# Eight block loads of each weight pair: from two with each of four pieces to one about every second piece

## The chip, the cores and the metric

The kernel runs on one core of one Trainium2 chip, in one launch. The metric is the device time in microseconds (us); before the change it is 2352.64 us, the median of three runs (2350.16 to 2354.2).

The core's engines run side by side and each works through its own list in order: PE multiplies matrices, ACT (ScalarE) and DVE (VectorE) do elementwise work, POOL (GpSimd) issues DMA transfers that add to their destination, SP (SyncE) issues nearly all other transfers. An instruction waits on semaphores until what it needs is there. A transfer that SP cannot issue yet holds up all those behind it.

## The reference, cut to what matters

A trunk of two layers on x of 256 tokens by 2048, in float32. Each layer adds a mixer and an MLP; the change touches the two MLPs.

```python
def squared_relu_mlp(h, w_up, w_down):
    u = jnp.einsum('bsd,df->bsf', h, w_up)
    return jnp.einsum('bsf,fd->bsd', jnp.square(jax.nn.relu(u)), w_down)

for layer in range(2):
    x = x + mixer(rms_norm(x, norm_mix[layer]))        # layer 0: windowed attention and Mamba-2, layer 1: dilated attention
    x = x + squared_relu_mlp(rms_norm(x, norm_ffn[layer]), w_up[layer], w_down[layer])
```

w_up is 2048 x 8192 and w_down 8192 x 2048, so each MLP reads 134 MB of weights.

## The kernel before

The kernel streams all weights from HBM through SBUF. Its work is a list, `plan`, of pieces. A piece is two k-tiles (2 x 128 rows) by up to 512 columns of a weight: a tile of 128 x 1024 float32, 512 KB. ACT writes a rounded copy of it (`whi`), DVE the rest (`wlo` = tile - `whi`), and PE multiplies the high and low parts with the high and low parts of the activations, three products in place of one, which keeps float32 accuracy.

There are two sorts of pieces.

- A plain piece (`Unit`) has its tile `wraw` from a ring of four, and takes 12 matmuls of 512 columns into `acc`. The MLP's w_up is done so ("up pieces").
- A pair piece belongs to a `Seven`. It takes the product of 1024 rows and 1024 columns of w_down as a 2 x 2 block product in seven multiplications rather than eight (Winograd's form of Strassen's scheme). Its four weight blocks "11", "12", "21", "22" come in two halves h of 512 KB each, so eight loads `sraw`. The seven multiplications P1, P2, Q3, Q7, Q6, Q5, Q4, two halves each, make 14 pieces of 6 matmuls into banks `sp`, which DVE adds to the residual `res` (`evict`). Sums of blocks that the scheme needs are made in place: by DVE (`add`), and by four accumulating DMAs that POOL issues (`accumulate`): block 22 onto "12" as soon as "12" is loaded, and block 12 onto "11" after P1 has been split.

Each MLP has seven periods c. In the first six, a first pair (columns 0 to 1023) and a second pair (1024 to 2047) are spread among 18 or 19 up pieces by `mixed`: first about five up pieces alone, then pair pieces and up pieces in turn, about two to one. The seventh has one pair among pieces of w_down. That makes 13 pairs a layer, 26 in all, with 208 loads and 104 accumulates.

The order on every engine is written out by hand: the loop in `run` goes over the list once, and at step i it records `low(i + 2)` (DVE), `fetch(i + 6)` (SP), `high(i + 3)` (ACT), `add(i + 4)` (DVE), and PE's matmuls of piece i. So SP's order of transfers is the order of the `fetch` calls, while each transfer goes out as soon as its buffer is free. A `wraw` buffer is free when DVE has split its fourth predecessor. The `sraw` buffers come from a pool of 31 that activations and intermediate results share. Before the change, `fetch` of a pair's piece issues loads with P1 and P2 only: "12" and "11" with either half of P1, "21" and "22" with either half of P2.

Nearly all instructions show line 71, a helper that records them; the SP loads are at L260 (`sraw`) and L307 (`wraw`), the accumulates at L274.

Of the kernel before, what the change touches and what calls it, by code (L numbers as in the profile page):

```python
# [20 lines left out]
W = 512  # L21
KC = 2
# [18 lines left out]
def trunk(ctx: ExitStack, tc: tile.TileContext, x, norm_mix, norm_ffn, w_up, w_down, ab_w_in, ab_q_norm,  # L41
          ab_k_norm, ab_sinks, ab_conv_w, ab_conv_b, ab_dt_bias, ab_a_log, ab_d_skip, ab_gate_norm,
          ab_w_out, c_w_qkv, c_q_norm, c_k_norm, c_w_o, shapes, out):
    nc = tc.nc
# [38 lines left out]
    def aux(name):  # L83
        return auxs.tile([128, W], F32, name=name, tag="aux")

    def f32(ap):
        return ap.bitcast(F32)
# [12 lines left out]
    def load_x(j):  # L100
        nc.sync.dma_start(res[:, :, j * W:(j + 1) * W], xt[:, :, j * W:(j + 1) * W])
# [85 lines left out]
    def need(label):  # L187
        while label not in done:
            assert step(True) or label in done, label
# [43 lines left out]
    def unit(*a, **k):  # L233
# [3 lines left out]

    SEVEN = (("P1", "a", "11"), ("P2", "b", "21"), ("Q3", "d", "22"), ("Q7", "c", "12"), ("Q6", "a", "22"),
             ("Q5", "a", "11"), ("Q4", "c", "21"))
    LOADS = {"P1": ("12", "11"), "P2": ("21", "22")}  # L240
    SUMS = {"Q6": ("22", "11", "22"), "Q4": ("21", "21", "22")}

    class Seven:
# [10 lines left out]
            self.raw[b, h] = t = work.tile([128, KC, W], F32, name="sraw", tag="w4")  # L254
            return t

        def fetch(self, p, h):
            for b in LOADS.get(SEVEN[p][0], ()):
                r, c = self.rows[int(b[0]) - 1] + h * KC, self.c0 + (int(b[1]) - 1) * W
                nc.sync.dma_start(self.tile(b, h),  # L260
                                  self.w[r * 128:(r + KC) * 128, c:c + W].rearrange("(k p) c -> p k c", p=128))
                if b == "12":
                    self.accumulate("12", 1, h)

        def add(self, p, h):
            if SEVEN[p][0] in SUMS:
# [25 lines left out]
    def run():  # L292
        todo = plan
        raws, parts = {}, {}

        def fetch(i):
            if i >= len(todo):
                return
            u, c = todo[i]
            if isinstance(u, Seven):  # L300
                u.fetch(*c)
                return
            kt = u.ktiles[c][0]
            raws[i] = raw = wpool.tile([128, KC, u.n], F32, name="wraw", bufs=RAW)
            o = 0
            for w, c0, m in u.segs:
                nc.sync.dma_start(raw[:, :, o:o + m],  # L307
                                  w[kt * 128:(kt + KC) * 128, c0:c0 + m].rearrange("(k p) c -> p k c", p=128))
                o += m

        def add(i):
            if i < len(todo) and isinstance(todo[i][0], Seven):
                todo[i][0].add(*todo[i][1])

        def high(i):
            if i < len(todo):
                u, c = todo[i]
                if isinstance(u, Seven):
                    raws[i] = u.source(*c)
                raw = raws[i]  # L320
                hi = wpool.tile([128, KC, raw.shape[2]], F32R, name="whi", bufs=AHEAD + 2)
                S.activation(hi, raw, AF.Copy)
                parts[i] = [hi]

        def low(i):
            if i < len(todo):
                raw = raws.pop(i)
                lo = wpool.tile([128, KC, raw.shape[2]], F32R, name="wlo", bufs=AHEAD + 1)
                V.tensor_tensor(lo, raw, f32(parts[i][0]), op=OP.subtract)
                parts[i].append(lo)  # L330
                u, c = todo[i]
                if isinstance(u, Seven) and c[0] == 0:
                    u.accumulate("11", 0, c[1])

        for i in range(RAW):
            if i % 2 == 0:
                load_x(i // 2)
            fetch(i)
        for i in range(AHEAD):
            high(i)  # L340
            low(i)
            if i == 0:
                need(todo[0][0].needs[0])
            if i % 2 == 0:
                load_x(2 + i // 2)
            fetch(RAW + i)
        high(AHEAD)
        nc.sync.dma_start(cst[:, C_TRI:], shapes[:, C_TRI:C_M0])
        nc.sync.dma_start(mask0, shapes[:, C_M0:C_M1])
        pending = []  # L350
        before = ps = None
        kept, held = [], []
        for i, (u, c) in enumerate(todo):
            if i:
                low(i + AHEAD - 1)
                fetch(i + AHEAD - 1 + RAW)
                high(i + AHEAD)
                add(i + AHEAD + 1)
            for f in pending:
                f()  # L360
            pending = []
            hi, lo = parts.pop(i)
            if isinstance(u, Seven):
                p, h = c
                name, b, _ = SEVEN[p]
                if p in u.needs and h == 0:
                    need(u.needs[p])
                new = b not in u.bank
                if new:
                    u.bank[b] = aux("sp")  # L370
                sp = u.bank[b]
                xh, xl, th, tl = u.operands(name)
                tick(True)
                for k in range(KC):
                    q = h * KC + k
                    wh, wl = xh[:, q, th:th + 128], xl[:, q, tl:tl + 128]
                    PE.matmul(sp, wh, hi[:, k], start=new and k == 0, stop=False, skip_group_check=True)
                    PE.matmul(sp, wh, lo[:, k], start=False, stop=False, skip_group_check=True)
                    PE.matmul(sp, wl, hi[:, k], start=False, stop=q == u.halves * KC - 1, skip_group_check=True)
                if h == u.halves - 1:  # L380
                    pending.append(lambda u=u, p=p: u.evict(p))
                    if p == 6:
                        done.add(u.mark)
                continue
            segs, ktiles, flip, n = u.segs, u.ktiles, u.flip, u.n
            if c == 0:
                if before is not None:
                    need(before)
                before = ps and id(ps)
                ps = [accs.tile([128, W], F32, name="acc") for _ in range(2)]  # L390
                kept.append(ps)
            if c in u.needs:
                need(u.needs[c])
            end = i == len(todo) - 1
            for k in range(KC):
                tick()
                first, last = c + k == 0, c + k == len(ktiles) - 1
                xh, xl, j = ktiles[c + k][1]()
                xh, xl = xh[:, j], xl[:, j]
                if flip:  # L400
                    for b in range(n // 128):
                        o = ps[b // 2][:, (b % 2) * T:(b % 2 + 1) * T]
                        wh, wl = hi[:, k, b * 128:(b + 1) * 128], lo[:, k, b * 128:(b + 1) * 128]
                        PE.matmul(o, wh, xh, start=first and b % 2 == 0, stop=False, skip_group_check=True)
                        PE.matmul(o, wh, xl, start=False, stop=False, skip_group_check=True)
                        PE.matmul(o, wl, xh, start=False, stop=last, skip_group_check=True)
                else:
                    rows = [(t, k, xh, xl) for t in range(2)]
                    if end:
                        held += rows  # L410
                        rows = sorted(held, key=lambda r: r[:2]) if last else []
                    for t, q, xh, xl in rows:
                        o = ps[t][:, :n]
                        h, l = xh[:, t * 128:(t + 1) * 128], xl[:, t * 128:(t + 1) * 128]
                        PE.matmul(o, h, hi[:, q], start=first, stop=False)
                        PE.matmul(o, h, lo[:, q], start=False, stop=False)
                        PE.matmul(o, l, hi[:, q], start=False, stop=last and q == k)
            if c + KC >= len(ktiles):
                pending.append(lambda u=u, ps=ps: u.after(ps))
                if u.mark is not None:  # L420
                    done.add(u.mark)
        for f in pending:
            f()
# [727 lines left out]

    mlp(1, n3, None, last=store)
    run()


# [47 lines left out]
```

## Time and profile before

| | |
|---|---|
| median of three runs | 2352.64 us |
| profiled execution | 2353.53 us, its span 2351.7 us |
| mean granted TensorE clock | 0.988 |
| PE, DVE, ACT, POOL busy | 2279.3, 1785.0, 1294.3, 133.8 us |
| read from HBM | 475.17 MB, 203 GB/s over the span |
| block loads by SP | 208 of 512 KB, median 9.1 us from issue to landing |
| accumulates by POOL | 104 of 512 KB, median 9.7 us |
| w_up tiles by SP | 256 of 512 KB, median 4.8 us |

ACT splits the first block of a pair at 535.6 us and the last at 2323.0 us. In a row of waits stand who waits, for whom, the total in us, how many times, and the longest; in a row of stretches the length, the busy time of each engine with its instructions, the granted share of the TensorE clock, the mean busy share of the 16 DMA engines and what they moved. Matmuls are pipelined: one is shown as busy for about 0.39 us while the next starts 0.23 us after it.

### The profile page before, as it was taken

To read this page: it belongs to the slowest core of one execution; us is meant where nothing else is said; L and a number is where in the kernel's file an instruction comes from. 1 tells how busy PE (TensorE), PEld (TensorE's weight loads), DVE (VectorE), ACT (ScalarE), POOL (GpSimd) and SP (SyncE) were. 2 spreads that over 40 slices of the span, in tenths; PEclk is the share of its full clock that TensorE was granted. 3 is DMA by queue.
4 is the path that set the end of the run, shared out by engine and by line. 5 is a ranking of instruction groups with operands and counts; after the bars stand their busy time and mean duration, and the time that the engine had idled before them with its cause. 6 is when DMAs were issued, how large, how long until landed. Compare 5 with 4: busy or idle time off the path is not lost.

```text
span 2351.7 us, 30275 instructions
## 1 busy us (share of the span) xinstructions
PE 2279.3 (97%) x11005; PEld 1882.3 (80%) x11005; DVE 1785.0 (76%) x2534; ACT 1294.3 (55%) x1627; POOL 133.8 (6%) x124
## 2 busy tenths in 40 slices
PE   8999999999999999999999999999999999999999
PEld 7999988888877878777788778778877877778777
DVE  6779886558887978778876776755687888878786
ACT  6565555446555655555554555554565555555553
POOL 1000000001000011001000000000101001011000
PEclk9999999999999999999999999999999999999999
DMA  7546555569687696878656455446969688696973
GB/s 229 163 136 196 179 179 183 186 192 291 189 238 224 193 290 175 254 214 251 179 168 189 159 154 177 155 162 187 277 174 285 188 235 247 167 298 183 272 204 128
DMA packets 257782, 479.29 MB, mean 204 GB/s; under 512 B 17316, under 2 KB 28112, under 8 KB 257632
## 3 DMA queue, kind: packets, MB, share of 16 engines
q1 hardware_dynamic: 219264, 416.34, 54.7%
q0 software_dynamic: 28800, 54.68, 13.0%
q10 hardware_dynamic: 9568, 6.34, 0.9%
q8 instruction: 86, 1.41, 0.2%
q14 instruction: 64, 0.52, 0.1%
HBM read 475.17 MB, written 2.13 MB: 203 GB/s over the span
## 4 chain that ended last, share of the span: by engine, by line
PE 82%; DMA 12%; DVE 4%; ACT 1%; issue 1%; SPq 0%; ACTq 0%; DVEq 0%
PE acc L71 59%; PE sp L71 17%; DMA sraw<-in_w_down_dram 6%; DMA wraw<-in_w_up_dram 5%; DVE wlo L71 2%; PE uT L71 1%; PE sc L71 1%; DVE res L71 1%; PE o L71 1%; ACT whi L71 1%; PE pT L71 1%; PE yp L71 1%; DMA wraw<-in_ab_w_in_dram 1%; PE xT L71 0%; DVE sraw L71 0%
## 5 line engine op out<-in xcount | busy, mean ns | idle before, releaser
L71 DVE TENSOR_TENSOR wlo<-wraw,whi 128x1024 fp32r<-128x1024 f32 (+1 forms) x584 | 705.4, 1215 | 259.7 <-PE acc L71 151.2
L71 ACT ACTIVATE whi<-wraw 128x1024 fp32r<-128x1024 f32 (+1 forms) x584 | 614.4, 1054 | 518.1 <-PE acc L71 291.8
L71 PE MATMUL acc<-whi,hThi 128*128 128x512 f32 (+1 forms) x1632 | 654.4, 401 | 12.8 <-ACT whi L71 10.7
L71 PE MATMUL acc<-wlo,hThi 128*128 128x512 f32 (+1 forms) x1632 | 640.1, 392 | 6.6 <-DVE wlo L71 6.5
L71 PE MATMUL acc<-whi,hTlo 128*128 128x512 f32 (+1 forms) x1632 | 639.9, 392 | 0.6 <-DVE hTlo L71 0.6
L71 ACT ACTIVATE whi<-sraw 128x1024 fp32r<-128x1024 f32 x364 | 382.3, 1059 | 345.8 <-DVE sraw L71 117.4
L71 DVE TENSOR_TENSOR wlo<-sraw,whi 128x1024 fp32r<-128x1024 f32 x364 | 443.7, 1222 | 124.4 <-ACT whi L71 48.4
L71 PEld LDWEIGHTS acc<-whi,hThi 128*128 128x128 f32 x1632 | 310.7, 190 | 81.1 <-ACT whi L71 13.9
L71 PEld LDWEIGHTS acc<-wlo,hThi 128*128 128x128 f32 x1632 | 310.8, 190 | 70.7 <-DVE wlo L71 10.5
L71 PEld LDWEIGHTS acc<-whi,hTlo 128*128 128x128 f32 x1632 | 309.8, 190 | 66.0 <-DVE hTlo L71 1.5
L274 POOL DMA_DIRECT2D sraw<-in_w_down_dram x104 | 125.3, 1208 | 2134.5 <-DMA sraw<-in_w_down_dram 1215.4
L71 PE MATMUL sp<-whi,sh 128*128 128x512 f32 x416 | 165.0, 397 | 22.4 <-DVE res L71 22.4
L71 PE MATMUL sp<-wlo,sh 128*128 128x512 f32 x416 | 164.3, 395 | 0.4
L71 PE MATMUL sp<-whi,sl 128*128 128x512 f32 x416 | 163.6, 393 | 0.0
L71 DVE TENSOR_TENSOR res<-res,sp 128x512 f32<-128x512 f32 x208 | 140.2, 684 | 25.5 <-PE sp L71 24.2
L71 DVE TENSOR_TENSOR sraw<-sraw 128x1024 f32<-128x1024 f32 x104 | 126.9, 1220 | 0.0
L71 PEld LDWEIGHTS sp<-whi,sh 128*128 128x128 f32 x416 | 79.0, 190 | 44.8 <-ACT whi L71 23.7
L71 PE MATMUL acc<-hThi,whi 128*128 128x256 f32 x384 | 112.5, 293 | 0.0
L71 PE MATMUL acc<-hTlo,whi 128*128 128x256 f32 x384 | 108.7, 283 | 0.0
L71 PE MATMUL acc<-hThi,wlo 128*128 128x256 f32 x384 | 108.7, 283 | 0.0
L71 PEld LDWEIGHTS sp<-wlo,sh 128*128 128x128 f32 x416 | 79.0, 190 | 18.5 <-DVE wlo L71 2.6
L71 PEld LDWEIGHTS sp<-whi,sl 128*128 128x128 f32 x416 | 79.2, 190 | 16.5
(227 smaller groups left out, 2790.5 us busy)
## 6 DMA issues: line engine op xcount, KB each, us to landing
wraw<-in_w_up_dram SPq DMA_DIRECT2D x256, 512.0 KB, 4.8
sraw<-in_w_down_dram SPq DMA_DIRECT2D x208, 512.0 KB, 9.1
sraw<-in_w_down_dram POOLq DMA_DIRECT2D x104, 512.0 KB, 9.7
wraw<-in_ab_w_in_dram SPq DMA_DIRECT2D x96, 512.0 KB, 3.7
wraw<-in_c_w_qkv_dram SPq DMA_DIRECT2D x96, 512.0 KB, 4.0
wraw<-in_ab_w_out_dram SPq DMA_DIRECT2D x48, 512.0 KB, 3.6
wraw<-in_w_down_dram SPq DMA_DIRECT2D x48, 512.0 KB, 4.0
wraw<-in_c_w_o_dram SPq DMA_DIRECT2D x32, 512.0 KB, 3.7
```

The source lines that it names most:

```text
L71: return f(out, *a, **k)
L274: nc.gpsimd.dma_start(self.raw[b, h], self.w[r * 128:(r + KC) * 128, c:c + W].rearrange("(k p) c -> p k c", p=128), accum_op=OP.add)
```

## The change

The table LOADS now names the eight loads one by one, with the step at which each is issued, counted from the pair's first piece: "11" half 0 at -12, "11" half 1 at -10, "21" at -8 and -6, "12" at -5 and -3, "22" at -2 and 0. `run` finds each pair's first piece in the list and notes the loads by step; in the step they stand after the `fetch` of the piece six ahead. `fetch` of a pair's piece does nothing now. The accumulate onto "12" is still recorded right behind the load of "12".

```diff
-    LOADS = {"P1": ("12", "11"), "P2": ("21", "22")}
+    LOADS = (("11", 0, -12), ("11", 1, -10), ("21", 0, -8), ("21", 1, -6), ("12", 0, -5), ("12", 1, -3), ("22", 0, -2),
+             ("22", 1, 0))
...
-        def fetch(self, p, h):
-            for b in LOADS.get(SEVEN[p][0], ()):
-                r, c = self.rows[int(b[0]) - 1] + h * KC, self.c0 + (int(b[1]) - 1) * W
-                nc.sync.dma_start(self.tile(b, h),
-                                  self.w[r * 128:(r + KC) * 128, c:c + W].rearrange("(k p) c -> p k c", p=128))
-                if b == "12":
-                    self.accumulate("12", 1, h)
+        def fetch(self, b, h):
+            r, c = self.rows[int(b[0]) - 1] + h * KC, self.c0 + (int(b[1]) - 1) * W
+            nc.sync.dma_start(self.tile(b, h), self.w[r * 128:(r + KC) * 128, c:c + W].rearrange("(k p) c -> p k c", p=128))
+            if b == "12":
+                self.accumulate("12", 1, h)
...
+        blocks = {}
+        for i, (u, c) in enumerate(todo):
+            if isinstance(u, Seven) and c == (0, 0):
+                for b, h, o in LOADS:
+                    blocks.setdefault(i + o, []).append((u, b, h))
...
             if isinstance(u, Seven):
-                u.fetch(*c)
                 return
...
+            for w, b, h in blocks.get(i, ()):
+                w.fetch(b, h)
```

PE, ACT, DVE and POOL have the same instructions in the same order before and after. Only SP's order differs. Its rows for the second period of layer 0 (c = 1), from the end of the period before to past the first pair's loads, were these (`sraw` is a block load, `wraw` an up tile):

```order
L307 DMA wraw<-in_w_up_dram 128x2x512 x10
L260 DMA sraw<-in_w_down_dram 128x2x512 x4
L307 DMA wraw<-in_w_up_dram 128x2x512
L260 DMA sraw<-in_w_down_dram 128x2x512 x4
L307 DMA wraw<-in_w_up_dram 128x2x512 x6
```

They are now:

```order
L310 DMA wraw<-in_w_up_dram 128x2x512 x5
L260 DMA sraw<-in_w_down_dram 128x2x512
L310 DMA wraw<-in_w_up_dram 128x2x512 x2
L260 DMA sraw<-in_w_down_dram 128x2x512
L310 DMA wraw<-in_w_up_dram 128x2x512 x2
L260 DMA sraw<-in_w_down_dram 128x2x512
L310 DMA wraw<-in_w_up_dram 128x2x512
L260 DMA sraw<-in_w_down_dram 128x2x512 x2
L310 DMA wraw<-in_w_up_dram 128x2x512
L260 DMA sraw<-in_w_down_dram 128x2x512 x2
L310 DMA wraw<-in_w_up_dram 128x2x512
L260 DMA sraw<-in_w_down_dram 128x2x512
```

Three of the eight loads have moved ahead of the tenth up tile, which stood right before all eight; the other five stand among the next tiles, two, two and one. For the second pair of the same period SP had eight loads in two blocks of four:

```order
L307 DMA wraw<-in_w_up_dram 128x2x512 x6
L260 DMA sraw<-in_w_down_dram 128x2x512 x4
L307 DMA wraw<-in_w_up_dram 128x2x512
L260 DMA sraw<-in_w_down_dram 128x2x512 x4
L307 DMA wraw<-in_w_up_dram 128x2x512 x10
```

and now has, from behind the first pair's last load on:

```order
L310 DMA wraw<-in_w_up_dram 128x2x512 x3
L260 DMA sraw<-in_w_down_dram 128x2x512
L310 DMA wraw<-in_w_up_dram 128x2x512
L260 DMA sraw<-in_w_down_dram 128x2x512 x2
L310 DMA wraw<-in_w_up_dram 128x2x512
L260 DMA sraw<-in_w_down_dram 128x2x512 x2
L310 DMA wraw<-in_w_up_dram 128x2x512
L260 DMA sraw<-in_w_down_dram 128x2x512 x2
L310 DMA wraw<-in_w_up_dram 128x2x512
L260 DMA sraw<-in_w_down_dram 128x2x512
```

Its first load follows the third up tile behind the first pair's last load, and four up tiles stand among its eight loads where one did.

## The prediction

> **What bounds the kernel now.** I read the page's first lines, then what PE waits for, then a table of stretches around every place where it waits, and last the DMA work there.
>
> ```profile
> span 2351.7 us, 30275 instructions
> PE 2279.3 (97%) x11005; PEld 1882.3 (80%) x11005; DVE 1785.0 (76%) x2534; ACT 1294.3 (55%) x1627; POOL 133.8 (6%) x124
> PE sp L71 <- DVE res L71: 22.4, 16, 2.4
> PE acc L71 <- ACT whi L71: 10.7, 9, 2.7
> PE sp L71 <- DVE wlo L71: 6.7, 9, 0.8
> PE acc L71 <- DVE wlo L71: 6.5, 9, 0.8
> PE uT L71 <- ACT relu L71: 4.8, 2, 4.3
> PE sp L71 <- ACT whi L71: 4.3, 3, 2.9
> ACT whi L71 <- DMA wraw<-in_w_up_dram: 77.6, 32, 7.3
> ACT whi L71 <- DMA sraw<-in_w_down_dram: 69.0, 30, 7.0
> ```
>
> TensorE is busy 97% of the span. What it waits for falls in two kinds: 22.4 us for evictions of a pair's bank (res), and 33.0 us (10.7 + 6.7 + 6.5 + 4.8 + 4.3) for weights that ACT and DVE have not yet split, or for an ACT op queued behind such a split. ACT in its turn waits 146.6 us for weights of these two stages to land. So there is DMA behind the second kind. The next table has ten stretches, one for each period of the two MLPs but the first of each, just where a period's first pair begins. The columns are length, PE busy, granted clock, DMA share and GB/s; two of the ten rows are left out, the sum holds them.
>
> ```profile
> 646.00:662.00 16.00, 11.65 (x33) 0.68 0.78 233
> 744.00:758.00 14.00, 9.31 (x33) 0.88 0.94 283
> 841.00:856.00 15.00, 12.07 (x43) 0.89 0.89 263
> 944.00:956.00 12.00, 9.68 (x39) 1.00 0.95 298
> 1046.00:1056.00 10.00, 7.11 (x28) 1.00 0.95 313
> 1782.00:1796.00 14.00, 8.85 (x28) 0.76 0.77 239
> 1879.00:1895.00 16.00, 11.64 (x36) 0.68 0.82 241
> ...
> 2179.00:2188.00 9.00, 6.67 (x25) 1.00 1.01 332
> sum 126.00, PE 92.58; mean PE 9.26
> ```
>
> PE idles 126.00 - 92.58 = 33.4 us there: all of the second kind. And in five of them the granted clock drops after the pause; at half clock the loss is (1 - clock) x length, 5.1 + 1.7 + 1.7 + 3.4 + 5.1 = 16.9 us. That the slow part is real shows in the chain of work (start, length), in the last two rows of the next fence: twelve matmuls took 5.06 us at 656 and 2.76 us at 664.
>
> ```profile
> 624.70 7.05 DMA sraw<-in_w_down_dram
> 631.81 21.23 DMA wraw<-in_w_up_dram
> 656.32 5.06 PE acc L71 x12
> 664.57 2.76 PE acc L71 x12
> ```
>
> The rows above them say why: a tile of w_up, issued at 631.81, landed 21.23 us later, where the usual is 4.8:
>
> ```profile
> wraw<-in_w_up_dram SPq DMA_DIRECT2D x256, 512.0 KB, 4.8
> sraw<-in_w_down_dram SPq DMA_DIRECT2D x208, 512.0 KB, 9.1
> sraw<-in_w_down_dram POOLq DMA_DIRECT2D x104, 512.0 KB, 9.7
> 620.00:625.00 5.00, 5.00 (x26) 4.15 (x25) 4.58 (x5) 3.68 (x4) 0.00 (x0) 1.00 0.30 97
> 630.00:635.00 5.00, 5.00 (x24) 4.15 (x23) 4.96 (x7) 1.49 (x2) 2.28 (x2) 1.00 1.05 374
> 640.00:645.00 5.00, 5.00 (x24) 4.14 (x23) 2.47 (x3) 1.06 (x1) 1.20 (x1) 1.00 1.10 261
> 650.00:655.00 5.00, 3.17 (x7) 1.86 (x7) 2.58 (x3) 2.32 (x4) 0.00 (x0) 0.59 1.05 385
> 655.00:660.00 5.00, 4.90 (x14) 3.74 (x15) 4.13 (x5) 4.63 (x6) 0.00 (x0) 0.50 0.46 132
> ```
>
> The last two columns are DMA share and GB/s. Before 625 the DMA engines are a third used; from 625 to 655 they are full; after it idle again. A 0.524 MB tile alone takes 0.524/385 = 1.36 us; while POOL's accumulating transfers run, the rate falls to 261, so one of them and one plain tile take 4.0 us together. The burst is eight block loads, four accumulates and, by SP's order, six w_up tiles: 4 x 4.0 + 10 x 1.36 = 29.6 us and some 4 us of first latency, from 624 to 657, as the table shows. This is a queue, not a lack of bandwidth: over the span the mean is 203 GB/s (the table ahead of this).
>
> **The change, part by part.** PE, ACT, DVE and POOL keep their orders; SP issues the same loads in other places. Nothing is added.
>
> ```profile
> L71 DVE TENSOR_TENSOR wlo<-wraw,whi 128x1024 fp32r<-128x1024 f32 (+1 forms) x584 | 705.4, 1215 | 259.7 <-PE acc L71 151.2
> L71 ACT ACTIVATE whi<-wraw 128x1024 fp32r<-128x1024 f32 (+1 forms) x584 | 614.4, 1054 | 518.1 <-PE acc L71 291.8
> ```
>
> (a) The burst. Of a first pair's eight loads, three (11 both halves, 21 first half) now stand before the up tile that opens the burst (issued at about 624), in the stretch that is a third used. That takes 3 x 1.36 = 4.1 us from the burst. More counts for the tile that PE paused for: behind the opening tile it was 11th (1, four loads, 1, four loads, itself) and is now 7th. Until about 635 transfers run at the plain rate, so 5 more land after the first (at 628), and the 7th about one shared step of 4.0 later, at 639, not 653. PE is busy without a break to 645 and has about two pair pieces (2 x 1.4, half of 2.76 each) ahead of it, so wants it at 648 or so; ACT and DVE need 1.05 + 1.22 us (the rows above) before that, so it is some 7 us early. Bounds: above, all of 33.4 + 16.9 less about 2.5 where the half clock lies in a pause and is counted twice, 48; below, each window's loss less 4.1 alone, which leaves 5.4 + 2.3 + 0.5 + 4.4 + 5.4 = 18, so a gain of 32. I take 46, near the upper end, because of the place in the queue.
>
> (b) What follows a pause. DVE had nothing to split meanwhile, and has to catch up; some 20 us later an eviction comes late.
>
> ```profile
> 867.00:877.00 10.00, 7.62 (x29) 0.83 1.08 305
> 2001.00:2011.00 10.00, 7.62 (x29) 0.83 1.08 313
> sum 31.00, PE 21.92; mean PE 5.48
> 822.00:876.00 54.00, 48.69 (x202) 38.71 (x201) 39.78 (x40) 28.80 (x32) 7.22 (x6) 0.94 1.00 295
> 1056.00:1080.00 24.00, 23.13 (x103) 18.85 (x102) 22.44 (x23) 14.77 (x17) 2.41 (x2) 1.00 0.81 246
> ```
>
> In four such stretches (two shown, with the sum of all four) PE idles 9.1 us. Where DVE is not behind, the same wait is 24.00 - 23.13 = 0.87 us (last row), so 3.5 of it stays: 5.6 us, and 2 x 0.17 x 10 = 3.4 of half clock, can go. Bounds 0 and 9; I take 5, because DVE has much to do there (39.78 of 54 us, third column of busy time).
>
> (c) Costs. A load stands in SP's queue ahead of w_up tiles that were first before. In the stretch ahead of the burst this delays one by 1.36 us at most, where the engines stand idle two thirds of the time. Each block holds its buffer some six pieces longer; where SP waited for a buffer it was short:
>
> ```profile
> SPq L260 <- PE acc L71: 8.0, 13, 2.7
> ```
>
> By the program's own waits nearly all loads in their new place need a buffer that was free long before in this trace. No row shows PE waiting for this, so the cost lies between 0 and, if every second pair lost one such 2.7 us, 12 x 2.7 = 32. I take 1, since 8.0 us over 13 waits is the nearest row and none of it is seen among PE's waits.
>
> Sum: 46 + 5 - 1 = 50 us. The profiled execution took 2353.53 us, 0.9 above the median of 2352.64: 2352.64 - 50 = 2302.6.
>
> The Trainium skill, "TensorE: Matmul & The Clock Gate", Part 1, has the clock fall to half after at least one idle window of about 3.4 us. The rows at 867 and 2001 show it after 2.38 us of idling, so the measurement decides here. By that rule the short pauses (744, 841, 867, 2001) would cost no clock, 6.8 us less, and the time would be about 2309.
>
> **Rivals.**
> 1. The burst is only shortened. The remaining five loads, four accumulates and the same w_up tiles still fill the engines for 25 us. Then (a) is 32, (b) 0: 2352.6 - 31 = 2321.6. For it speaks the share of 1.05 to 1.10; against it the 7 us of lead.
> 2. DVE becomes the bound where PE no longer pauses. Ten of the res waits that are 0.87 now would become those of 867:877 (2.38 and 1.7 of clock): 10 x 3.2 = 32, and the time 2334.6. For it: 22.44 of 24 us busy. Against it: in just that row PE lost only 0.87.
> 3. No change: the bytes are the same, and what leaves the burst meets the end of the last pair's burst, so the transfers are late anyway: 2352. Against it: 0.30 of DMA share before 625. The Trainium skill, "DMA: Bandwidth & Descriptors", "Issuing engines are not separate DMA queues", has all queues interleave on the same 16 engines; the 261 GB/s beside the accumulates agrees.
> 4. Slower: a second pair's loads now go out right behind the first pair's burst, and SP, issuing in order, stands at one of them for a buffer while w_up tiles queue behind it. If each of the 12 second pairs then paused as 744:758 does (4.7 and 1.7 of clock), that is 77 us, and the time 2352.6 - 50 + 77 = 2380. It decides from eight such pauses on. Against it: the short SP waits.
>
> **How the numbers follow.** Forecast 0.66, rival 1 0.17, rival 2 0.08, rival 3 0.05, rival 4 0.04. Faster is the first three, 0.91; within 0.2% (4.7 us, about what a measurement of this kernel can tell) 0.05; slower 0.04. The low end is both upper bounds with no cost and a few more of the res waits gone, 2290; the high end takes in rival 1 and half of what lies between it and rival 2, 2330.
>
> **What would show it.** In the changed profile: no PE idling beyond 1 us where each period's first pair begins; PE's waits for whi, wlo and relu down from 33.0 to under 6; ACT's wait for block loads from 69.0 to under 15; the mean clock up from 0.988 to about 0.995; block loads landing in 5 to 7 us at the median, not 9.1. Res waits should stay near 16 in number and drop to about 17 us. If ACT still waits tens of us for w_up, (a) is wrong in its place in the queue; if res waits grow, rival 2; if SP waits long at the block loads, rival 4.

## The result: 71 us faster, and the profile after

The changed kernel took 2282.23 us (median; 2280.56 to 2284.88), the kernel before 2353.42 us beside it: a ratio of 0.970 with a 95% interval of 0.968 to 0.972, that is 71.2 us less. The forecast was 50 us less, with 2290 as the low end, so the time lies 8 us below the range. The profiled executions are 2353.53 and 2280.56 us, 73.0 apart in the time and 72.9 in the span; the accounts below are made on these. One of the runs below, of the kernel without accumulates, took 2383.80 us at a mean clock of 0.900 where all others have 0.986 or more, and its median and ratio leave that run out.

The first lines of the page of the kernel after, its chain's shares by engine, and two rows of its DMA issues (the last number is the median from issue to landing):

```profile
span 2278.8 us, 30296 instructions
PE 2245.9 (99%) x11005; PEld 1868.2 (82%) x11005; DVE 1787.9 (78%) x2534; ACT 1303.1 (57%) x1627; POOL 134.1 (6%) x124
...
PE 97%; DVE 1%; ACT 1%; issue 0%; DMA 0%; SPq 0%; DVEq 0%; ACTq 0%
...
wraw<-in_w_up_dram SPq DMA_DIRECT2D x256, 512.0 KB, 5.9
...
sraw<-in_w_down_dram SPq DMA_DIRECT2D x208, 512.0 KB, 8.1
```

With the same number of matmuls, PE is busy 33.4 us less, and idle 39.5 us less (72.4 before, 32.9 now). DMA has gone from the chain that sets the end, which had these shares before:

```profile
PE 82%; DMA 12%; DVE 4%; ACT 1%; issue 1%; SPq 0%; ACTq 0%; DVEq 0%
```

The waits after, PE's two largest and ACT's two for weights of the MLPs' up and block loads (total, times, longest):

```profile
PE sp L71 <- DVE res L71: 16.8, 16, 2.3
PE pp L71 <- DMA cst<-in_shapes_dram: 2.9, 1, 2.9
...
ACT whi L71 <- DMA wraw<-in_w_up_dram: 9.1, 9, 1.9
...
ACT whi L71 <- DMA sraw<-in_w_down_dram: 0.7, 3, 0.3
```

PE no longer waits for whi, wlo or relu at all (33.0 us before); ACT waits 9.8 us for the two kinds of tiles where it waited 146.6. Here is the same work as in the ten windows of the prediction, from and to the same matmuls but for the windows at 1013.50 and 2112.10, which begin 0.8 us of work earlier (columns: length, PE busy, granted clock, DMA share, GB/s; two rows are left out, the sum holds them):

```profile
645.30:652.00 6.70, 6.70 (x33) 1.00 1.10 260
734.00:740.90 6.90, 6.90 (x35) 1.00 1.10 261
823.80:833.10 9.30, 9.30 (x43) 1.00 1.09 279
918.00:926.00 8.00, 8.00 (x39) 1.00 1.09 269
1013.50:1020.40 6.90, 6.90 (x34) 1.00 1.10 268
1744.90:1750.60 5.70, 5.70 (x28) 1.00 1.10 266
1833.60:1840.70 7.10, 7.10 (x35) 1.00 1.09 264
...
2112.10:2118.30 6.20, 6.20 (x31) 1.00 1.10 259
sum 69.70, PE 69.70; mean PE 6.97
```

PE has no gap and the full clock, and yet the DMA engines are as full as in the burst before (shares of 1.09 to 1.11) and move 259 to 279 GB/s, the rate beside accumulates. The burst is still there; it no longer holds what PE needs next.

### The profile page after: what moved, and what is told of

It reads as the page before. It is cut to its first block, busy times and chain, and to the rows that moved or that the text cites. A ratio compares the mean times of both kernels' runs of the same rounds, so it can differ in the third digit from the quotient of the medians.

```text
span 2278.8 us, 30296 instructions
## 1 busy us (share of the span) xinstructions
PE 2245.9 (99%) x11005; PEld 1868.2 (82%) x11005; DVE 1787.9 (78%) x2534; ACT 1303.1 (57%) x1627; POOL 134.1 (6%) x124
## 4 chain that ended last, share of the span: by engine, by line
PE 97%; DVE 1%; ACT 1%; issue 0%; DMA 0%; SPq 0%; DVEq 0%; ACTq 0%
PE acc L71 69%; PE sp L71 21%; PE uT L71 1%; PE sc L71 1%; PE o L71 1%; PE pT L71 1%; DVE res L71 1%; PE yp L71 1%; DVE wlo L71 1%; PE xT L71 0%; DMA wraw<-in_ab_w_in_dram 0%; ACT whi L71 0%; PE qp L71 0%; PE yo L71 0%; PE kp L71 0%
## 5 line engine op out<-in xcount | busy, mean ns | idle before, releaser
L71 PE MATMUL acc<-whi,hThi 128*128 128x512 f32 (+1 forms) x1632 | 647.9, 397 | 1.8 <-ACT hThi L71 1.8
L71 PE MATMUL acc<-wlo,hThi 128*128 128x512 f32 (+1 forms) x1632 | 633.7, 388 | 0.0
L71 PE MATMUL sp<-whi,sh 128*128 128x512 f32 x416 | 163.2, 392 | 16.8 <-DVE res L71 16.8
```

Source lines behind the costliest of these rows:

```text
L71: return f(out, *a, **k)
```

## Experiments

All ratios are to the kernel before, run beside each. The theory: a w_up tile is late by its place in SP's queue behind the block loads, times the step of that queue, which is long while POOL accumulates. The main rivals: spreading the loads is enough by itself; or it is the engines' total work there that counts.

### The loads twelve pieces ahead, still in twos

The grouping and order of before, but every load goes out twelve pieces ahead, where it was six. This is lead without spreading; all loads but the first get more lead than the change gives them, which issues the last one with the pair's first piece.

```diff
             if isinstance(u, Seven):
-                u.fetch(*c)
                 return
...
+            if i + 12 < len(todo) and isinstance(todo[i + 12][0], Seven):
+                todo[i + 12][0].fetch(*todo[i + 12][1])
```

> The lead alone: two loads with each of four pieces as before, but issued 12 pieces ahead, not six. Theory (the place in SP's queue): four loads now stand ahead of the up tile that opens the burst, and the tile that PE waited for is 7th behind it, as in the changed kernel, so no pause is left and the time is that of the changed kernel, 2282 us within 6. Rival (the spreading counts: loads two at a time are still a burst): half of the pauses or more stay, 2310 to 2353 us.

Measured 2291.28 us, ratio 0.974 (0.972 to 0.976): a gain of some 62 us, a little outside what the theory gave. Its two largest waits of PE, and ACT's for w_up tiles:

```profile
PE sp L71 <- DVE res L71: 16.8, 16, 2.3
PE uT L71 <- ACT relu L71: 5.0, 3, 2.6
...
ACT whi L71 <- DMA wraw<-in_w_up_dram: 33.7, 17, 5.6
```

All ten places are free of pauses. What it lacks against the change is the second row: ahead of each layer's first period the DMA engines have less room (shares of 0.69 and 0.81 from 520 to 530 in the kernel before, where it is 0.30 at 620), the loads in twos and the accumulates behind them push the w_up tiles back, PE waits for relu, and the same matmuls take 3.3 and 4.2 us longer there. So lead alone gives nearly all, and the change's table some 9 us more.

### The loads spread, without the lead

One load with each of eight pieces, from six ahead on.

```diff
+    LOADS = (("11", 0, -6), ("11", 1, -5), ("21", 0, -4), ("21", 1, -3), ("12", 0, -2), ("12", 1, -1), ("22", 0, 0),
+             ("22", 1, 1))
```

> The spreading and the order alone: one load with each piece from six pieces ahead, in the order 11, 11, 21, 21, 12, 12, 22, 22. No load stands ahead of the opening up tile; the tile that PE waited for is 8th behind it (11th before, 7th in the changed kernel). Theory (place in the queue): it lands one shared step of 4 us later than in the changed kernel, which the lead of about 7 us covers, so most of the gain is there: 2283 to 2300 us. Rival (the lead counts, the loads must fall into the quiet stretch): 2335 to 2353 us.

Measured 2318.44 us, ratio 0.985 (0.983 to 0.987), half of the gain, which neither side had expected. PE's largest wait, ACT's largest for a weight, and the landing of the accumulates:

```profile
PE sp L71 <- DVE res L71: 29.5, 24, 2.9
...
ACT whi L71 <- DMA sraw<-in_w_down_dram: 62.4, 23, 7.8
...
sraw<-in_w_down_dram POOLq DMA_DIRECT2D x104, 512.0 KB, 12.6
```

The w_up tiles come in time now: at the ten places PE has no pause, and the matmuls there take as long as in the changed kernel. But the blocks don't: ACT waits 62.4 us for them, and DVE, behind ACT, then evicts late (29.5 us over 24 waits, not 16.8 over 16), nearly all of it later in the pairs. The fourth accumulate of the second period lands at 755.5, 17.7 us after its issue. Two reasons were open: the block "12", on which accumulates wait, stood late in the table (four pieces later than in the kernel before); or all loads lacked the lead.

### Spread as before, with block 12 first

The two reasons apart: the same eight places, other order.

```diff
+    LOADS = (("12", 0, -6), ("11", 0, -5), ("12", 1, -4), ("11", 1, -3), ("21", 0, -2), ("21", 1, -1), ("22", 0, 0),
+             ("22", 1, 1))
```

> As the experiment with one load a piece from six pieces ahead, but with each half of 12 ahead of that of 11, as in the kernel before, so that the accumulates start as early as there. If what was left over in that experiment (36 us short of the change) came from accumulates that landed late, because 12 was loaded late, this one is faster than its 2318 us: 2285 to 2300. If it came from the missing lead, it stays at 2318 us or above, up to 2340, since the accumulates take their share of the engines early again.

Measured 2322.78 us, ratio 0.988 (0.986 to 0.989). The accumulates land as soon after their issue as in the kernel before (9.7 us, not 12.6), and it is no better.

```profile
PE sp L71 <- DVE res L71: 24.8, 19, 2.6
PE sp L71 <- DVE wlo L71: 9.4, 13, 0.8
...
ACT whi L71 <- DMA sraw<-in_w_down_dram: 101.0, 43, 5.5
...
sraw<-in_w_down_dram POOLq DMA_DIRECT2D x104, 512.0 KB, 9.7
```

ACT waits still longer for block loads (101.0 us, 43 times), and the loss has moved: 26.4 of the 40.9 us that the profiled execution lacks against the changed kernel lie at the ten places again. So late accumulates weren't the whole reason. What both tables share is little lead, at the end above all: their last load goes out a piece after the pair's first, where the kernel before had all eight out two pieces ahead of it. The next experiment, whose loads start at the same piece and are all out two pieces ahead, does better.

### The order of blocks alone

The kernel before, with 11 and 21 in the first two pieces and 12 and 22 in the last two; number and places of the loads as they were.

```diff
-    LOADS = {"P1": ("12", "11"), "P2": ("21", "22")}
+    LOADS = {("P1", 0): ("11", "21"), ("P1", 1): ("11", "21"), ("P2", 0): ("12", "22"), ("P2", 1): ("12", "22")}
...
-            for b in LOADS.get(SEVEN[p][0], ()):
+            for b in LOADS.get((SEVEN[p][0], h), ()):
```

> The order alone: two loads with each of the same four pieces as before, but 11 and 21 first, 12 and 22 after them. The tile that PE waited for stays 11th behind the opening one. Theory with the place alone: no change, 2345 to 2355 us. Theory with the sharing (what slows the queue is POOL's accumulates, and they can't start before a block 12 has landed, now 7th and not 2nd): the 11th transfer still goes at the plain rate and lands near 641, in time, so 2285 to 2305 us.

Measured 2297.25 us, ratio 0.976 (0.974 to 0.978): 57 us from a change in which as many loads stand ahead of each w_up tile as before. Place alone doesn't make the lateness, then; the step does. With block 12 in the last two pieces, the first accumulate of the second period goes out at 637.46 (629.88 before), and the tile that PE had waited for lands at 642.3, near the 641 expected.

```profile
PE sp L71 <- DVE res L71: 24.3, 20, 2.3
...
ACT whi L71 <- DMA sraw<-in_w_down_dram: 41.4, 14, 5.5
ACT whi L71 <- DMA wraw<-in_w_up_dram: 41.1, 30, 3.3
```

### No accumulates

The kernel before with all loads where they were, and POOL's 104 accumulating transfers left out.

```diff
-                if b == "12":
-                    self.accumulate("12", 1, h)
...
-                if isinstance(u, Seven) and c[0] == 0:
-                    u.accumulate("11", 0, c[1])
```

> The kernel before without its 104 accumulating transfers (two block sums of each pair are left out). All loads are where they were. If the sharing with the accumulates makes the queue late: ten transfers of 1.36 us behind the first, the tile PE waited for lands near 641 and not 653, the pauses go, 2285 to 2300 us. If the eight loads in one place make it late by themselves: 2335 to 2353 us.

Measured 2282.48 us, ratio 0.970 (0.967 to 0.972): the whole gain, without moving a load. PE's largest wait, and stretches of its trace (length, busy PE, PEld, DVE, ACT, POOL, clock, DMA share, GB/s):

```profile
PE sp L71 <- DVE res L71: 16.8, 16, 2.3
...
640.00:645.00 5.00, 5.00 (x24) 4.14 (x23) 4.91 (x5) 2.79 (x4) 0.00 (x0) 1.00 1.05 387
645.00:650.00 5.00, 5.00 (x25) 4.13 (x24) 3.83 (x5) 3.84 (x5) 0.00 (x0) 1.00 0.57 169
```

The burst runs at 387 GB/s (before, 261 in 640 to 645), the tile lands at 643.4, and all is over before 650, not at 657. Without the long step, the old places do no harm. This run also leaves out 11% of the bytes, and ACT no longer waits for accumulated blocks, so by itself it doesn't show that the slow step was the cause; the order alone, where nothing is left out, points the same way.

### The change for first pairs only, and for second pairs only

A condition on the column decides which pairs follow the new table; the others load as before. The second kernel has `!=` there.

```diff
+            if isinstance(u, Seven) and c == (0, 0) and u.c0 == 0:
```

> The change for the first pairs of the periods alone (12 of 26); the second pairs' loads are issued two with each of four pieces as before. Theory (only where a first pair's loads meet the plain up tiles did PE pause): the whole gain, 2282 us within 6. Rival (the second pairs' loads take part in the lateness, or a load behind the first pair's burst costs something): 2300 to 2335 us, or below 2276 if the change there costs.

> The change for the second pairs alone (14 of 26, the lone pair of the seventh period among them). Theory: no gain, 2353 us within 6. Rival: 2315 to 2340 us. If early second loads push back tiles that the first pair's stretch still needs, slower, 2360 us or more.

First pairs only: 2283.35 us, ratio 0.970 (0.968 to 0.971), the whole gain. Second pairs only: 2352.79 us, ratio 1.001 (0.999 to 1.002), nothing. The latter's waits are much like those of the kernel before:

```profile
PE acc L71 <- ACT whi L71: 9.6, 6, 3.9
...
ACT whi L71 <- DMA wraw<-in_w_up_dram: 85.8, 31, 7.0
```

The second pairs' moved loads cost nothing that these runs can tell either (the interval is 2 us less to 5 us more), which the prediction had left between 0 and 32 us.

### Three loads ahead, and one

Only "11" both halves and "21" first half go ahead of the burst, at the change's places; the other five stand where the old table had them.

```diff
+    LOADS = (("11", 0, -12), ("11", 1, -10), ("21", 0, -8), ("12", 0, -6), ("12", 1, -5), ("22", 0, -3), ("21", 1, -2),
+             ("22", 1, -2))
```

> Only the three loads of the prediction's step (a) are moved ahead (11 at -12 and -10, 21 half 0 at -8); the other five are issued where they were, two or three together. The tile PE waited for is 8th behind the opening one (7th in the changed kernel, 11th before). Theory: the three account for all of it, 2282 to 2290 us. Rival (the spreading of the other five is needed too): 2300 to 2330 us.

Then only the first half of "11" ahead, and seven as they were:

```diff
+    LOADS = (("11", 0, -12), ("12", 0, -6), ("12", 1, -5), ("11", 1, -5), ("21", 0, -3), ("22", 0, -3), ("21", 1, -2),
+             ("22", 1, -2))
```

> One load alone (11 half 0 at -12) is moved ahead, seven stay where they were; the tile PE waited for is 10th. Theory: one transfer less in the queue is 1.36 to 4 us less at each of the ten places, so a part of the gain, 2315 to 2340 us. Rival with a threshold (the queue is so full that one load less does nothing): 2345 to 2353 us; or, if the lead of the first block alone is what PE lacked: 2290 us or less.

Three ahead: 2282.93 us, ratio 0.971 (0.969 to 0.972). One ahead: 2339.53 us, ratio 0.995 (0.994 to 0.996). The waits with three ahead:

```profile
PE sp L71 <- DVE res L71: 18.6, 16, 2.3
...
ACT whi L71 <- DMA wraw<-in_w_up_dram: 34.7, 17, 4.5
```

and with one:

```profile
PE sp L71 <- DVE res L71: 19.8, 16, 2.4
PE acc L71 <- ACT whi L71: 11.9, 6, 4.4
PE uT L71 <- ACT relu L71: 11.5, 7, 4.4
...
ACT whi L71 <- DMA wraw<-in_w_up_dram: 89.6, 25, 7.0
```

Three loads moved give all of it; the places of the other five are worth nothing that the runs can tell. With three ahead ACT still waits 34.7 us for w_up tiles, but PE never for whi, wlo or relu: the lateness has shrunk to what ACT and DVE have in hand. One load takes 13.4 us (8 to 15) of the 71. That isn't in proportion (a third would be 24). A lateness that costs PE nothing once it is below some slack would do that; this is a reading, not shown.

### A faster kernel: one evicting piece earlier

The one wait left of any size is PE's for an eviction, 16.8 us. In the changed kernel, the last two pieces of a pair change places.

```diff
-             ("Q5", "a", "11"), ("Q4", "c", "21"))
+             ("Q4", "c", "21"), ("Q5", "a", "11"))
```

> The changed kernel with Q4 ahead of Q5 in the order of the seven products, so that bank a is not taken up by Q5 right behind the eviction of Q6; the same products and sums. PE's 16 waits for evictions, 16.8 us in the changed kernel, come from this order: 14 of 0.87 us as shown, some 1.03 us each from start to start, go, and the time is 2282 - 14 = 2268 us within 5. Rival: the wait moves, since Q5's eviction is then the pair's last and the next pair's bank or the next eviction waits for it: 2278 to 2290 us.

Measured 2264.33 us, ratio 0.962 (0.960 to 0.963), 18 us below the change. PE's three largest waits:

```profile
PE acc L71 <- DVE ul L71: 5.2, 2, 2.6
PE pp L71 <- DMA par<-in_norm_mix_dram: 2.9, 1, 2.9
PE acc L71 <- ACT hThi L71: 2.7, 2, 2.1
```

The row for res is gone: 16.8 us, of which 2.8 come back as a longer wait for ul (2.4 before). The two profiled executions are 15.4 us apart. With the same evictions to do, DVE no longer makes PE wait for res, so these waits came from the order of pieces. This is the fastest version tried.

## Where the prediction held, and the term that was too small

**What bounds the kernel: right.** PE paused for w_up tiles that stood behind block loads in one queue. First pairs alone carry the gain, and three loads moved ahead are enough, as the prediction had it. The tile that landed at 653.04 in the kernel before, forecast for 639, now lands at 636.9. In the experiments it lands at 634.3 (twelve ahead in twos), 642.3 (order alone), 643.4 (no accumulates), 644.9 (three ahead) and 651.5 (one ahead); in the first four PE has no pause at that place, in the last it idles 4.7 us. One thing the forecast of 639 passed over: the change also moves block 12 from first to fifth, so the first accumulate goes out at 632.05, not 629.88, and lands at 641.5, behind the tile; no shared step of 4.0 us stands before it. Three loads ahead with block 12 right behind them, and the order alone, each give most or all of the gain; the change does both, and the runs don't divide its gain between them.

**(a) The burst: the term that was too small.** Here a step of the prediction failed. I took each pause at the idle time that the rows show, 33.4 us in all, added 16.9 for the clock, and put the upper bound at 48 and the term at 46. Compared matmul by matmul, the same work at the ten places takes 58.6 us less. In the five places that ran at full clock 19.3 us went, where 12.2 of idle are shown: 7.1 us stood in no row that I had read. In the other five 39.4 us went, where 21.5 of idle and 17.1 of clock are shown. There the double count was real, since 3.3 us of the clock's loss lie inside shown pauses, but pauses that read too short make up for it. So the losses counted were too few, and the 2 us that I stayed below the bound came on top. The reason is how pauses are shown. Five matmuls around two pauses in the trace of the kernel before (start, length, in brackets the idle shown):

```profile
1977.81 0.39 PE L71 MATMUL sp<-wlo,uh 128*128 128x512 f32 x1
1978.04 0.39 PE L71 MATMUL sp<-whi,ul 128*128 128x512 f32 x1
1979.02 0.51 PE L71 MATMUL acc<-whi,hThi 128*128 128x512 f32 x1 [0.59 <-ACT whi L71]
1980.28 0.50 PE L71 MATMUL acc<-wlo,hThi 128*128 128x512 f32 x1 [0.76 <-DVE wlo L71]
1980.62 0.40 PE L71 MATMUL acc<-whi,hTlo 128*128 128x512 f32 x1
```

Matmuls overlap: where nothing is waited for, the next starts 0.23 us later (the first two rows), though each shows 0.39. From the second row to the last, three steps take 2.58 us where they would take 0.69, so PE lost 1.89 us; 0.59 and 0.76, together 1.35, are shown as idle. Each of the two pauses reads 0.27 us short. The five places at full clock have 20 pauses, which makes 5.4 of the 7.1 us; the rest is not placed.

**(b) What follows a pause: right in kind, too small.** The same four stretches:

```profile
844.00:851.00 7.00, 6.13 (x30) 1.00 1.06 276
...
1943.00:1950.00 7.00, 6.13 (x29) 1.00 1.06 262
...
sum 22.50, PE 19.01; mean PE 4.75
```

31.00 became 22.50, 8.5 us (8.7 matmul by matmul) where I took 5 of at most 9. The idle left is 0.87 us in each, just the value that I had read off the row at 1056:1080; so what was off is the discount for DVE's load.

**Not in the sum: 4.8 us of clock.** At two places at the end of a layer's periods, with pauses for res, uh and ul that stay, the kernel before ran at half clock for four stretches, the changed one for one. First before, then after (shorter windows around the pauses for uh and ul):

```profile
1115.00:1133.00 18.00, 13.76 (x47) 0.81 0.75 209
2248.00:2266.00 18.00, 13.80 (x47) 0.81 0.81 219
```

```profile
1088.00:1096.00 8.00, 6.07 (x21) 0.79 1.00 291
2186.00:2192.00 6.00, 4.07 (x17) 1.00 0.96 313
```

By the rows, the loss of clock was 0.19 x 18 x 2 = 6.8 us and is 0.21 x 8 = 1.7; the same matmuls take 4.8 us less. Whether this is the change's doing the runs don't show: the profiles of the kernels above have one to four such stretches at the same pauses, the one with second pairs alone changed, which keeps its pauses at the ten places, two. Without these 4.8 us the time would still lie below the range.

**(c) Costs: none that the runs can tell, where I took 1.** The kernel with second pairs alone changed shows it.

The sum, in the profiles: 58.6 + 8.7 + 4.8 = 72.1, and 0.7 more at the start and in the first periods, is 72.8 of the 72.9.

**The signs that I had named.** PE's waits for whi, wlo and relu under 6: none. ACT's for block loads under 15: 0.7. Res waits 16, about 17 us: 16, 16.8. Clock about 0.995: 0.999. Block loads landing in 5 to 7 us: 8.1, wrong. The engines stay full beside the accumulates, and a load that is asked for earlier need not land faster; why it is 8.1 was not tried.

**The rivals.** 1, a burst only shortened: no pause is left, and 2321.6 is 39 us off. The kernels that spread without lead come out near it (2318 and 2323), but by chance: what they lose is time in which ACT waits for block loads. 2, DVE becomes the bound: res waits fell from 22.4 to 16.8. 3, no change, since the engines are full anyway: they are as full, and it doesn't matter, since PE's tile is no longer at the back. 4, second pairs' loads block the queue: changed alone, they are worth 1.001 (0.999 to 1.002).

## What to carry to other kernels

In a queue that issues in order, what stands behind a burst is late by its place times the step, and here the step went from 1.36 to 4.0 us where an accumulate ran beside it: look which tile the bound engine waits for, count what stands ahead of it, and move just so many loads into a stretch where the engines idle. Spreading the burst over the time in which it is needed gave half here; starting it earlier gave nearly all. When you price pauses of a pipelined engine, take start to start of its instructions, and add the half clock and the late evictions that follow.

## What the runs showed of the hardware that I had not expected

The half clock isn't a fixed answer to a pause. In one execution, the changed kernel's, two stretches with the same 1.93 us of idle PE shown (8.00 - 6.07 and 6.00 - 4.07, a wait of 0.74 for uh and one of 1.19 for ul in each; the wait before them, 2.31 for res, is the same too) end one at 0.79 and one at 1.00. The Trainium skill, "TensorE: Matmul & The Clock Gate", Part 1, has half clock after at least one idle window of about 3.4 us; here it came once after less and once not, so that rule doesn't settle which pause costs clock. The four timed runs, with mean clocks from 0.997 to 0.999, differ by 4.3 us, and 0.002 of 2280 is 4.6.

And an accumulate costs more than its bytes. Beside plain loads it takes, by an estimate from 385 and 261 GB/s, 4.0 - 1.36 = 2.6 us more of the DMA engines, twice what a plain tile of its size takes. Leaving out all 104 of 512 KB (54 MB, 11% of what the program moves) is worth some 70 us with the loads in their old places. What leaving them out is worth in the changed kernel wasn't tried.
